# One layer of a hybrid decoder: the outputs of the DeltaNet heads are transposed in 32x32 blocks on VectorE and put in place by transfers through DRAM

## The chip, the cores and the metric

The kernel runs on one core of a Trainium2 chip. The time is that of one execution on the device, in microseconds (us). Before the change three runs gave 1203.46, 1204.15 and 1205.03; the median is 1204.15. The names of the engines are those of the profile: PE is the matrix engine (TensorE) and PEld its loads of weights, DVE is VectorE, ACT is ScalarE, POOL is GpSimd, SP is SyncE, which issues the transfers (SPq is its queue). L139 is line 139 of the kernel. Most instructions are recorded at a helper's line: L139 and L141 are the wrappers of the engines (L141 those with high priority), L191 is a product, L195 a transpose on PE, L200 a transpose of half a block.

## The reference, cut to what matters

The input has 1024 tokens of width 1024, all in float32. The layer is

```
h   = rmsnorm(x);  proj = h @ w_in
o_a = gated_delta_rule(q, k, v, g, beta)          # 4 heads of 128
o_a = rmsnorm(o_a, gdn_norm_w) * silu(z_a)        # per head and token
o_b = dilated_attention(q_b, k_b, v_b)            # 8 heads of 64
x   = x + concat(o_a, o_b) @ w_out
h   = rmsnorm(x);  u = causal_dwconv(h @ w_up)
x   = x + (silu(gate) * up) @ w_down
out = rmsnorm(x)
```

The change touches the second line of o_a: the output of each DeltaNet head is scaled per token by its norm and per feature by gdn_norm_w, multiplied by silu of a projection z, and enters the output projection.

## The kernel before, in words

Activations are held transposed: features on the 128 partitions, the 1024 tokens along the free dimension, in 8 chunks of 128. A product in full precision is made of three fast ones: both operands are split into a high part (a copy rounded to fp32r, on ACT) and a low part (the rest, on DVE: `split`, L209), and `mm3` (L203) multiplies high with high, low with high and high with low. I call these three products of 128x512 a triple. The weights come from DRAM as wst and are split into whi and wlo.

The program is written as generators that a planner (class Weave, L46) interleaves. It keeps a clock of PE and an estimate of when each tile is ready, by fixed and per-element costs for each engine (L148 to L156), and takes the stream with the lowest level that is ready. This gives PE a written order of instructions, which the hardware keeps. The order on DVE, ACT and SP is made afterwards by a scheduler with priorities; each engine then works in its order and waits where an operand is late.

Around the change there are these streams:

- `dense` (L505), level 9: the columns of the input projection, 128 outputs each, 2 halves of 512 tokens, 8 triples per half. It fills what the other streams leave. The last four columns are z, one per DeltaNet head. Each half is evacuated from PSUM by DVE with the token norm rstdB (`scaled`, L444): xr for z, aqkv for the attention.
- `chain` (L789), level 1: the recurrence of one DeltaNet head over 8 chunks of 128 tokens, all four heads interleaved. Each step goes PE, DVE (r, wke, the state ct), ACT (w, vtok) and back. Its output vtok has tokens on the partitions and, per chunk, 128 features along the free dimension. At the end ms holds the mean square per token, POOL raises it to the power -0.5 and multiplies vtok by it (L854, L855).
- `finish` (L858), level 1: for each head 8 transposes of 128x128 on PE, 4 into one PSUM bank, then a copy on ACT that scales each feature by gw2 (half of gdn_norm_w) into ot, and a transfer of each half to the DRAM tile mixer[h].
- In `dense`, when z of head h is reached, og is loaded from mixer[h] with one transfer (L548) and the gate is put off: `gate` (L481) makes zz = tanh(xr/2) on ACT, zz = (zz + 1) * xr on DVE, og = og * zz on DVE. With the halved gw2 this is the product with silu.
- `attention` (L904), level 5: scores on PE, softmax on DVE and ACT (sm), transposes of the probabilities on PE (L200), copies of these on DVE and ACT (pt, pb), products with the values, and oT on DVE.
- `mixer_splits` (L1087), level 0: splits og of each DeltaNet head and ot (the attention's outputs, back from mixer) into ohi and olo. They take the slots of xhi and xlo, so each waits for the last product of `dense` that reads that slot.
- `out_proj` (L1115), level 8: products of ohi and olo with the output weights, heads 0 to 3 first.

All transfers named here stand in one queue, SP's, which issues them in order: one that waits holds those behind it.

Of the kernel before, what the change touches and what calls it, by code (L numbers as in the profile page):

```python
# [7 lines left out]
F32 = mybir.dt.float32  # L8
F32R = mybir.dt.float32r
AF = mybir.ActivationFunctionType  # L10
OP = mybir.AluOpType
# [4 lines left out]
P = 128  # L16
# [3 lines left out]
NCH = 8  # L20
# [124 lines left out]
def hybrid_layer(tc, I, out):  # L145
    nc = tc.nc
    wv = Weave()
    ve = Engine(wv, nc.vector, "vector", 0.07, 0.00105)  # L148
    ac = Engine(wv, nc.scalar, "scalar", 0.12, 0.00085)
# [3 lines left out]
    po_ = Engine(wv, nc.gpsimd, "gpsimd", 0.15, 0.0021)  # L153
    sy = Engine(wv, nc.sync, "sync", 0.05, 0.00142, 2.2)

    sa = Engine(wv, nc.scalar, "sync", 0.05, 0.00142, 2.2)  # L156
    es = ExitStack()
    cp = es.enter_context(tc.tile_pool(name="cp", bufs=1))
# [2 lines left out]
    sp = es.enter_context(tc.tile_pool(name="sp", bufs=1))  # L161
# [3 lines left out]
    def tile_(pool, shape, dt, name, tag, bufs):  # L165
        return wv.slot(pool.tile(list(shape), dt, name=name, tag=tag, bufs=bufs), tag, bufs)
# [3 lines left out]
    def A(name, tag, dt=F32, shape=(P, 1024)):  # L170
        if tag in TURNS:
            i = turns[tag] = turns.get(tag, -1) + 1
            tag = TURNS[tag][i % len(TURNS[tag])]
        return tile_(lp, shape, dt, name, tag, SLOTS[tag])

    def X(name, dt=F32R):
        return A(name, "X", dt)

    def const(name, shape, src=None):
        t = cp.tile(list(shape), F32, name=name)  # L180
        if src is not None:
            sy.dma_start(t, src)
        return t
# [3 lines left out]
    def after(inst, anchor, reason="keeps a slot free until it is needed"):  # L187
        tc.add_manual_dep(inst.ins, anchor.ins.name, order, reason=reason)
# [5 lines left out]
    def tp(dst, src):  # L194
        tc.stamp_issue_order_token(nc.tensor.transpose(dst, src, ident).ins, TOKEN)  # L195
        wv.product(0.11, dst, src)
# [12 lines left out]
    def split(src, hi, lo):  # L209
        ac.activation(hi, src, AF.Copy)  # L210
        return ve.tensor_tensor(lo, src, hi.bitcast(F32), op=OP.subtract)

    def raw_weight(src, n=1024):
        st = tile_(wp, [P, n], F32, "wst", "wst", 2)
        sy.dma_start(st, src)
        return st
# [11 lines left out]
    def wk(src, st=None):  # L228
        return [t.rearrange("p (k m) -> p k m", k=KT) for t in weight(src, st=st)]
# [12 lines left out]
    mixer = dp.tile([8, P, S], F32, name="mixer")  # L242
# [10 lines left out]
    def bank(tag, name="ps"):  # L253
        return tile_(pp_, (P, 512), F32, name, tag, 2)

    def next_bank(tag, *tiles, slack=0.0):

        while max(wv.need(*tiles), wv.slot_free(tag, 2)) + slack > 1e-3:
            yield max(wv.need(*tiles), wv.slot_free(tag, 2)) + slack
        return bank(tag)  # L260

    def half(i):
        return slice(i * 512, i * 512 + 512)
# [80 lines left out]
    gw2 = const("gw2", [P, 1])  # L344
# [23 lines left out]
    rstdB = const("rstdB", [P, S])  # L368
# [75 lines left out]
    def scaled(pair, name, by_class=False, tag="ev", t=None, hs=(0, 1)):  # L444
        if t is None:
            t = A(name, tag)
        for h in hs:
            sl = half(h)
            if by_class:
                ve.tensor_tensor(t[:, sl].rearrange("p (n c u) -> p n u c", n=4, c=4),  # L450
                                        pair[h].rearrange("p (n u c) -> p n u c", n=4, c=4),
                                        rstdB[:, sl].rearrange("p (n u c) -> p n u c", n=4, c=4), op=OP.mult)
            else:
                ve.tensor_tensor(t[:, sl], pair[h], rstdB[:, sl], op=OP.mult)
        return t
# [22 lines left out]

    put_off = []

    def gate(og, xr, anchor=None):  # L481
        y = A("zz", "ev")
        insts = [ac.activation(y, xr, AF.Tanh, scale=0.5),
                 ve.scalar_tensor_tensor(y, y, 1.0, xr, op0=OP.add, op1=OP.mult),
                 ve.tensor_tensor(og, og, y, op=OP.mult)]
        last["og"] = insts[2:]
        if anchor is not None:
            after(insts[0], anchor[0], "the softmax goes first")
            after(insts[1], anchor[1], "the softmax goes first")
# [6 lines left out]
    gated = {}  # L496

    def first_keys():
        xr = [scaled(pst[2 * h:2 * h + 2], "xr", tag=("ev", "ev", "qa")[h]) for h in range(3)]
        for h in range(3):  # L500
            T["k", h] = conv_silu(xr[h], 4 + h, "kT", "kT*")
            wv.add(3, kprep(h))
            yield wv.need(T["k", h])

    def dense():  # L505

        yield from wv.until("first")
        yield from wv.until("norms")
        wv.add(2, first_keys())

        raw = [raw_weight(I["wi"][0])]
        nxt = wk(None, raw.pop())
        raw.append(raw_weight(I["wi"][1]))
        for i, col in enumerate(DENSE):
            kind, h = col[:2]
            if kind == "z":
                yield from wv.until(("o", h))
            w = nxt
            if i + 1 < len(DENSE):
                nxt = wk(None, raw.pop())  # L520
            if i + 2 < len(DENSE):
                raw.append(raw_weight(I["wi"][i + 2]))
            pair = []
            for hh in range(2):
                pt = bank("hf")
                yield wv.need(pt, *w)
                for k in range(KT):
                    mm3(pt, [t[:, k, :] for t in w], [t[:, half(hh)] for t in xs[k]], k == 0, k == KT - 1)
                    yield 0.0

                pair.append(pt)
                if hh == 0:
                    while put_off:
                        gate(*put_off.pop(0))
                    xr = A("aqkv" if kind == "a" else "xr", "go" if kind == "k" else "ev")
                scaled(pair, "xr", kind == "a", t=xr, hs=(hh,))
            if kind == "k":
                T["k", h] = conv_silu(xr, 4 + h, "kT", "kT*")
                wv.add(3, kprep(h))
            elif kind == "q":  # L540
                q = conv_silu(xr, h, "qT", "qa")
                wv.add(4, qprep(h, q))
            elif kind == "v":
                v = conv_silu(xr, 8 + h, "vT", "qa")
                wv.add(4, vprep(h, v))
            elif kind == "z":
                og = gated[h] = A("og", "kT*")
                sy.dma_start(og, mixer[h])  # L548
                if i + 1 < len(DENSE):
                    put_off.append((og, xr))  # L550
                else:
                    gate(og, xr)
            else:
                sy.dma_start(apark[h, col[2]], xr)
                wv.done.add(col)
        wv.done.add("dense")
# [299 lines left out]
        wv.add(1, finish(h, vtok))  # L856

    def finish(h, osb):  # L858
        for hh in range(2):
            pt = yield from next_bank("atr", osb, slack=0.8)  # L860
            for c in range(4):
                i = 4 * hh + c
                tp(pt[:, c * P:(c + 1) * P], osb[:, i * P:(i + 1) * P])
            ot = tile_(sp, [P, 512], F32, "ot", "t2", 2)
            ac.activation(ot, pt, AF.Copy, scale=gw2)
            sy.dma_start(mixer[h][:, half(hh)], ot)
        wv.done.add(("o", h))


# [208 lines left out]
    ots = {}  # L1078
# [4 lines left out]
    def load_residual(m):  # L1083
        x1[m] = A("x1", "kT")
        sy.dma_start(x1[m], I["xT"][m * P:(m + 1) * P, :])

    def mixer_splits():  # L1087
        yield from wv.until("dense")
        load_residual(MORDER[0])
        load_residual(MORDER[1])  # L1090
        wv.done.add("residual")
        for i in range(8):
            yield from wv.until(("o", i))
            ots[i] = (X("ohi"), X("olo"))
            if i < H:
                lo = split(gated[i], *ots[i])
                last.setdefault("olo", []).append(lo)
                if i and "probabilities" in last:
                    after(lo, last["probabilities"], "the probabilities go first")
            else:  # L1100
                src = A("ot", "ev")
                for h in range(2):
                    sl = half(h)
                    if i < 7 or h == 0:
                        sy.dma_start(src[:, sl], mixer[i][:, sl])
                    split(src[:, sl] if i < 7 or h == 0 else last["oT"], *[t[:, sl] for t in ots[i]])
            yield wv.need(*ots[i])
            wv.done.add(("ot", i))
# [656 lines left out]
```

## Time and profile before

| what | value |
|---|---|
| median of three runs | 1204.15 us |
| the profiled execution | 1202.61 us |
| its span | 1200.8 us |
| granted PE clock | 0.998 |
| ACT, share of the span | 48% |
| POOL, share of the span | 5% |
| transfers of mixer<-ot | 8 of 256 KB, 3.1 us to landing |
| transfers of og<-mixer | 4 of 512 KB, 4.2 us to landing |

The span is the time between the first and the last instruction in the trace; the execution is 1.81 us longer. A row of the timeline gives start, duration, engine, line, operation, output and inputs, the number of merged instructions and, in brackets, the idle time of the engine just before and what ended it. A row of a tile gives minimum, median and maximum duration in ns and the first and last start. Matmuls overlap, so their durations add up to more than the time they take.

### The profile page before, as it was taken

The page shows a single profiled execution, that of the slowest core. Times are in us where ns is not written, and L with a number is a line of the kernel's source. Part 1 is how long each engine was busy: PE and PEld are TensorE (multiplying, and loading weights), DVE is VectorE, ACT ScalarE, POOL GpSimd, SP SyncE. Part 2 cuts the span into 40 slices and gives each one's busy share as a digit, 9 for nine tenths or more (in the row PEclk, how much of TensorE's full clock was granted, in tenths as well). Part 3 has the DMA queues.
Part 4 walks back from the last instruction along what each step waited for, and adds up shares of the span by engine and source line. Part 5 has one row for each costly group of instructions (what it writes and reads, how often), then busy time and mean ns, then how long its engine had stood idle before and what let it go on. Part 6 is the DMA issues. An engine that isn't in the chain of part 4 may idle for free.

```text
span 1200.8 us, 18366 instructions
## 1 busy us (share of the span) xinstructions
PE 1190.4 (99%) x7058; PEld 986.1 (82%) x7058; DVE 956.5 (80%) x1532; ACT 575.3 (48%) x1129; POOL 57.1 (5%) x50
## 2 busy tenths in 40 slices
PE   9999999999999999999999999999999999999997
PEld 7888888898777778888888888888888888888887
DVE  7686985483666678767898988989898889898987
ACT  7383344364344445555544544444454454445452
POOL 0212010023000000000000000000000000000001
PEclk9999999999999999999999999999999999999999
DMA  6323234426442313443223222131222395356724
GB/s 237 106 75 102 83 115 129 150 85 238 134 134 84 115 58 124 166 141 122 69 72 106 74 85 102 56 106 53 106 86 72 98 377 217 113 183 218 241 98 157
DMA packets 81704, 152.72 MB, mean 127 GB/s; under 512 B 21552, under 2 KB 32592, under 8 KB 81616
## 3 DMA queue, kind: packets, MB, share of 16 engines
q1 hardware_dynamic: 80896, 151.02, 37.7%
q8 instruction: 55, 0.90, 0.3%
q10 hardware_dynamic: 720, 0.53, 0.1%
q14 instruction: 33, 0.27, 0.1%
HBM read 113.49 MB, written 35.93 MB: 124 GB/s over the span
## 4 chain that ended last, share of the span: by engine, by line
PE 96%; DVE 2%; ACT 1%; DMA 1%; issue 0%; POOL 0%; DVEq 0%; SPq 0%; ACTq 0%; POOLq 0%
PE ps L191 46%; PE pa L191 20%; PE dw L191 17%; PE pc L191 10%; PE ps L195 2%; PE ps L200 1%; DMA wst<-in_wu 0%; ACT sm L141 0%; DVE x1h L139 0%; DMA xt<-in_xT 0%; DVE sm L141 0%; DVE aqkv L139 0%; DVE T L139 0%; DVE wst L139 0%; DVE pair L139 0%
## 5 line engine op out<-in xcount | busy, mean ns | idle before, releaser
L191 PE MATMUL dw<-pr 128*128 128x512 f32 (+1 forms) x984 | 211.4, 376 | 0.0
L191 PEld LDWEIGHTS dw<-pr 128*128 128x128 f32 x984 | 176.7, 188 | 33.6
L191 PE MATMUL ps<-xhi,whi 128*128 128x512 f32 x448 | 184.5, 412 | 0.0
L191 PE MATMUL ps<-xhi,wlo 128*128 128x512 f32 x448 | 175.2, 391 | 0.0
L191 PE MATMUL ps<-xlo,whi 128*128 128x512 f32 x448 | 174.9, 390 | 0.1
L191 PE MATMUL pa<-T,pair 128*128 128x512 f32 x528 | 127.1, 389 | 0.2
L191 PEld LDWEIGHTS pa<-T,pair 128*128 128x128 f32 x528 | 99.0, 188 | 21.2 <-ACT u L139 0.7
L191 PEld LDWEIGHTS ps<-xhi,whi 128*128 128x128 f32 x448 | 84.3, 188 | 19.2 <-issue 3.6
L191 PEld LDWEIGHTS ps<-xhi,wlo 128*128 128x128 f32 x448 | 84.1, 188 | 18.4
L191 PEld LDWEIGHTS ps<-xlo,whi 128*128 128x128 f32 x448 | 84.4, 188 | 14.6 <-DVE xlo L139 0.4
L139 ACT ACTIVATE u<-pa 128x512 f32<-128x512 f32 x44 | 26.3, 598 | 109.7 <-PE pa L191 109.7
L139 DVE SCALAR_TENSOR_TENSOR y<-xu,fcw,y 128x1023 f32<-128x1023 f32 (+1 forms) x44 | 56.3, 1281 | 24.4 <-ACT y L139 24.4
L139 ACT ACTIVATE pr<-wd 128x1024 fp32r<-128x1024 f32 x33 | 35.0, 1061 | 76.1 <-DVE wd L139 39.5
L139 ACT ACTIVATE whi<-wst 128x1024 fp32r<-128x1024 f32 (+2 forms) x38 | 38.5, 1014 | 57.5 <-PE ps L191 48.3
L191 PE MATMUL pa<-B,A 128*128 128x512 f32 x264 | 63.5, 389 | 0.0
L191 PE MATMUL pa<-T,S 128*128 128x512 f32 x264 | 63.4, 389 | 0.0
L191 PE MATMUL pc<-B,pair 128*128 128x512 f32 x264 | 63.4, 389 | 0.0
L191 PE MATMUL pc<-T,S 128*128 128x512 f32 x264 | 63.4, 389 | 0.0
L139 DVE TENSOR_TENSOR wst<-wst 128x512 f32<-128x512 f32 x88 | 60.4, 686 | 0.8
L191 PE MATMUL ps<-B,pair 128*128 128x512 f32 x252 | 60.5, 389 | 0.0
L191 PEld LDWEIGHTS pc<-B,pair 128*128 128x128 f32 x264 | 49.6, 188 | 10.3
L191 PEld LDWEIGHTS pa<-T,S 128*128 128x128 f32 x264 | 49.6, 188 | 10.3
(244 smaller groups left out, 2234.7 us busy)
## 6 DMA issues: line engine op xcount, KB each, us to landing
wst<-in_wu SPq DMA_DIRECT2D x44, 512.0 KB, 3.5
wd<-in_wd SPq DMA_DIRECT2D x44, 512.0 KB, 4.3
wst<-in_wi SPq DMA_DIRECT2D x25, 512.0 KB, 3.6
upark<-y SPq DMA_DIRECT2D x22, 512.0 KB, 3.5
r<-upark SPq DMA_DIRECT2D x22, 512.0 KB, 9.4
apark<-aqkv SPq DMA_DIRECT2D x12, 512.0 KB, 2.8
wa<-in_wd SPq DMA_DIRECT2D x22, 256.0 KB, 2.9
wst<-in_wo SPq DMA_DIRECT2D x8, 512.0 KB, 3.9
```

The lines of the kernel that those rows point to most:

```text
L139: return getattr(eng, op)(*a, **kw)
L191: tc.stamp_issue_order_token(nc.tensor.matmul(dst, lhs, rhs, start=start, stop=stop, **kw).ins, TOKEN)
L195: tc.stamp_issue_order_token(nc.tensor.transpose(dst, src, ident).ins, TOKEN)
L200: tc.stamp_issue_order_token(nc.tensor.transpose(dst, src[rows], ident[rows, rows]).ins, TOKEN)
```

## The change

`finish` no longer uses PE and ACT. DVE transposes all of vtok at once in 32x32 blocks: within each block of 32 partitions and 32 elements, rows and columns are exchanged, and the blocks of one chunk are written so that ft holds, per partition, 4 groups of 256 elements. One transfer stores ft to mixer[h]. The blocks themselves are brought to their partitions by the load: og is now loaded with four transfers of 32 partitions, each from pieces of 256 elements (1 KB).

After this the tokens of og lie in another order along the free dimension: 4 groups of 32 within a chunk come first (`by_row`), where before they followed the token's number (`by_token`). So xr of a z column is written by DVE in that block order, the gate works in it, and the split into ohi and olo reads og by rows and writes the tokens back in their order, with a pattern of 4x8x32. The scaling by gw2 has moved into the last operation of the gate, which is a scalar_tensor_tensor now. The planner counts each of the four loads with 0.05 us + 0.00036 us per element (`sq_`). All else follows from the planner and the scheduler.

```diff
+    sq_ = Engine(wv, nc.sync, "sync", 0.05, 0.00036, 2.2)
...
+    def by_row(t):
+        return t.rearrange("p (a c i) -> p a c i", a=4, c=NCH)
+
+    def by_token(t):
+        return t.rearrange("p (c a i) -> p a c i", a=4, i=32)
+
     def gate(og, xr, anchor=None):
         y = A("zz", "ev")
         insts = [ac.activation(y, xr, AF.Tanh, scale=0.5),
                  ve.scalar_tensor_tensor(y, y, 1.0, xr, op0=OP.add, op1=OP.mult),
-                 ve.tensor_tensor(og, og, y, op=OP.mult)]
+                 ve.scalar_tensor_tensor(og, og, gw2, y, op0=OP.mult, op1=OP.mult)]
...
-                scaled(pair, "xr", kind == "a", t=xr, hs=(hh,))
+                if kind == "z":
+                    ve.tensor_tensor(by_row(xr)[:, :, 4 * hh:4 * hh + 4], by_token(pt), by_token(rstdB[:, half(hh)]), op=OP.mult)
+                else:
+                    scaled(pair, "xr", kind == "a", t=xr, hs=(hh,))
...
                 og = gated[h] = A("og", "kT*")
-                sy.dma_start(og, mixer[h])
+                for b in range(4):
+                    sq_.dma_start(og[32 * b:32 * b + 32].rearrange("j (a y) -> j a y", a=4),
+                                 mixer[h].rearrange("(a j) (b y) -> b j a y", a=4, b=4)[b])
...
     def finish(h, osb):
-        for hh in range(2):
-            pt = yield from next_bank("atr", osb, slack=0.8)
-            for c in range(4):
-                i = 4 * hh + c
-                tp(pt[:, c * P:(c + 1) * P], osb[:, i * P:(i + 1) * P])
-            ot = tile_(sp, [P, 512], F32, "ot", "t2", 2)
-            ac.activation(ot, pt, AF.Copy, scale=gw2)
-            sy.dma_start(mixer[h][:, half(hh)], ot)
+        yield wv.need(osb, slack=0.8)
+        t = A("ft", "kt")
+        ve.transpose(t.rearrange("p (b c i) -> p b c i", b=4, c=NCH), osb.rearrange("p (c b j) -> p b c j", c=NCH, b=4))
+        sy.dma_start(mixer[h], t)
         wv.done.add(("o", h))
...
             if i < H:
-                lo = split(gated[i], *ots[i])
+                g4, hi4, lo4 = by_row(gated[i]), by_token(ots[i][0]), by_token(ots[i][1])
+                ac.activation(hi4, g4, AF.Copy)
+                lo = ve.tensor_tensor(lo4, g4, hi4.bitcast(F32), op=OP.subtract)
```

## The prediction

> **What bounds the kernel now.** I read the page's busy times and its chain first, then the busy time by stretches.
>
> ```profile
> span 1200.8 us, 18366 instructions
> ...
> PE 1190.4 (99%) x7058; PEld 986.1 (82%) x7058; DVE 956.5 (80%) x1532; ACT 575.3 (48%) x1129; POOL 57.1 (5%) x50
> ...
> PE 96%; DVE 2%; ACT 1%; DMA 1%; issue 0%; POOL 0%; DVEq 0%; SPq 0%; ACTq 0%; POOLq 0%
> ```
>
> ```profile
> 225.00:271.00 46.00, 44.94 (x322) 41.33 (x321) 33.89 (x105) 27.33 (x108) 7.53 (x6) 1.00 0.30 101
> 425.00:470.00 45.00, 44.82 (x460) 34.81 (x457) 37.52 (x83) 21.32 (x53) 0.31 (x1) 1.00 0.20 63
> ```
>
> The columns of the second view are stretch, length, then the busy time of PE, PEld, DVE, ACT and POOL, and the granted clock. TensorE is busy 1190.4 of 1200.8 us, and 96% of the chain is its own. In the recurrence it is idle 1.06 us (46.00 less 44.94), in the end of the attention 0.18. So a matmul taken away is time saved, and there is no idle time on PE to hide a new wait in. PE runs in a fixed order: what makes one product late makes all later ones late.
>
> The profiled execution took 1202.61 us, 1.81 more than its span. The median of the three runs is 1204.15, 1.54 above it; I make the sum against the profiled execution and put it onto the median.
>
> **What goes from PE.**
>
> ```profile
> L195 PE MATMUL ps<-ident,vtok x32: 272/273/273, 271.1 to 297.5; 128*128 128x128 f32 x32
> L139 ACT ACTIVATE ot<-ps,gw x8: 667/688/692, 271.7 to 298.0; 128x512 f32<-128x512 f32 x8
> ```
>
> ```profile
> 296.78 1.04 PE L195 MATMUL ps<-ident,vtok 128*128 128x128 f32 x8
> 297.58 0.47 PE L191 MATMUL ps<-xhi,whi 128*128 128x512 f32 x1
> 297.89 0.39 PE L191 MATMUL ps<-xlo,whi 128*128 128x512 f32 x1
> 298.12 0.40 PE L191 MATMUL ps<-xhi,wlo 128*128 128x512 f32 x1
> ```
>
> A transpose shows 0.273 us, but they overlap: eight in a row hold PE from 296.78 to 297.58, and the step after them is 0.31 instead of 0.23. That is 0.80 + 0.08 = 0.88, or 0.11 each, and 32 x 0.11 = **3.5 us**. The eight copies on ACT (8 x 0.688 = 5.5 us) go too, but ACT is busy for only 48% of the span, and no wait of PE above ends with them, so I count nothing for them.
>
> The orders of the two built programs, set against each other, show what fills the holes: between the recurrence's steps stand single dense triples (three products of 0.23, 0.69 us) where the transposes were. That makes three more changes from the recurrence's fp32 products to the dense ones, 0.08 each: **+0.2**. Nine more triples stand ahead of the attention's start and eleven fewer behind its last product (13 before, 2 after).
>
> **What comes onto DVE.** Four block transposes of 128x1024. The trace has none, so I bound one from the nearest rows.
>
> ```profile
> L139 DVE TENSOR_TENSOR og<-og,zz x4: 1211/1214/1225, 429.2 to 472.4; 128x1024 f32<-128x1024 f32 x4
> L139 DVE TENSOR_TENSOR olo<-og,ohi x4: 1218/1222/1226, 465.2 to 474.7; 128x1024 fp32r<-128x1024 f32 x4
> L139 DVE TENSOR_TENSOR xr<-ps,rstdB x32: 677/691/692, 44.4 to 469.1; 128x512 f32<-128x512 f32 x32
> L139 DVE TENSOR_TENSOR aqkv<-ps,rstdB x24: 1036/1106/1146, 67.6 to 395.7; 128x512 f32<-128x512 f32 x24
> L141 DVE COPY pt<-ps x64: 263/415/425, 311.8 to 457.2; 128x256 f32<-128x256 f32 x56, 128x128 f32<-128x128 f32 x8
> ```
>
> ```profile
> 453.57 0.82 DVE L141 TENSOR_SCALAR sm<-sm,mx 128x448 f32<-128x448 f32 x2
> ```
>
> A plain pass over 1024 elements takes 1.22. The costliest pattern, aqkv's scatter of single elements, takes 1.106 for 512 against xr's 0.691, so 2.2 for 1024. The two scalings of sm, one input each, take 0.82 for 2 x 448, or 0.94 for 1024; that is the other end. I take 1.22, and 1.13 from start to start: its runs are 32 elements, and the copies of pt in runs of 64 (256 elements in 0.415) show no such penalty. The same choice stands for xr (0.69), the splits (1.22) and the gate's product (the same length with one more operand) in block order. [...]
>
> Where they stand decides. The first stands in DVE's order behind ms at 266.87 and ahead of vtok, aqkv and wke:
>
> ```profile
> 266.87 0.96 DVE L141 TENSOR_SCALAR ms<-ms 128x8 f32<-128x8 f32 x1 [0.27 <-ACT osq L141]
> 267.50 0.35 DVE L141 SCALAR_TENSOR_TENSOR vtok<-ps,gq,vtok 128x128 f32<-128x128 f32 x1
> 267.80 1.13 DVE L139 TENSOR_TENSOR aqkv<-ps,rstdB 128x512 f32<-128x512 f32 x1
> 268.76 0.33 DVE L141 TENSOR_SCALAR wke<-ps,ke 128x128 f32<-128x128 f32 x1
> 269.25 1.22 DVE L139 TENSOR_TENSOR wlo<-wst,whi 128x1024 fp32r<-128x1024 f32 x1
> 270.38 0.35 DVE L141 SCALAR_TENSOR_TENSOR ct<-ct,ge,ps 128x128 f32<-128x128 f32 x1
> ```
>
> ```profile
> 265.45 1.90 POOL L139 TENSOR_TENSOR vtok<-vtok,ms 128x1024 f32<-128x1024 f32 x1
> ...
> 269.63 2.59 POOL L139 TENSOR_TENSOR vtok<-vtok,ms 128x1024 f32<-128x1024 f32 x1
> ```
>
> ```profile
> 269.45 0.49 PE L191 MATMUL ps<-wke,ktok 128*128 128x128 f32 x2
> 270.79 0.49 PE L191 MATMUL ps<-ct,kT 128*128 128x128 f32 x2 [0.18 <-DVE ct L141]
> ```
>
> DVE has no gap from 267.5 to 270.6, and PE already waits there, for wke and then for ct. The transpose can start at 267.5, when POOL's product of head 0 is through. Everything behind it moves by 1.13, and PE's product on ct with it: **+1.1**.
>
> Then a second effect. POOL's second product took 2.59 instead of 1.90; it starts at 269.63, inside wlo (269.25 to 270.38): 0.69 too long, about what is left of wlo. The 0.96 of ms, an operation on 8 elements, fits the other direction: it waits for POOL's product to end at 267.35. So the two engines exclude each other for some operations. With wlo moved to 270.38, POOL comes first, 269.63 to 271.53, and wlo starts 1.15 later: ct is then at 272.65 and PE's product near 273.0 instead of 270.79: **+1.1** more. [...] If POOL does not hold wlo back, this term is 0; I keep 0 to 1.1.
>
> The second transpose stands ahead of vtok and r, and its input is ready by then; the extra triple in PE's order covers it (r at about 274.9, PE's product on it at 275.3). The third waits for POOL behind ms of head 2, PE reaches the next wke about 0.3 later than it is ready. The fourth follows POOL's last product and falls into the time where DVE idles for 5.26 us between the halves of a column:
>
> ```profile
> 299.94 1.15 DVE L139 TENSOR_TENSOR aqkv<-ps,rstdB 128x512 f32<-128x512 f32 x1 [5.26 <-PE ps L191]
> ```
>
> Together **+0.1**, at most 1.2 if one is not covered.
>
> **SP's queue.** Per head, one store instead of two and four loads of og instead of one; the first load waits for its store, and behind it stand weight loads.
>
> ```profile
> 290.20 0.38 SPq L139 DMA_DIRECT2D wst<-in_wi  x1
> ```
>
> ```profile
> wst<-in_wi SPq DMA_DIRECT2D x25, 512.0 KB, 3.6
> ```
>
> ```profile
> 299.70 1.06 ACT L139 ACTIVATE whi<-wst 128x1024 fp32r<-128x1024 f32 x1 [1.02 <-PE ps L191]
> ```
>
> The weight load at 290.20 lands 3.6 later, 5.9 us before its split. The issue at 290.20 takes 0.38, so three more are 1.1 us; og itself is first used at 429.2, by its row above. So 0; a load later than that would cost what exceeds the 5.9.
>
> **The end of the attention.** Thirteen dense triples (8.9 us) stand there now behind the last product of the attention; two (1.4 us) will.
>
> ```profile
> 456.24 1.41 DVE L141 COPY pt<-ps 128x256 f32<-128x256 f32 x4
> ...
> 469.07 0.69 DVE L139 TENSOR_TENSOR xr<-ps,rstdB 128x512 f32<-128x512 f32 x1 [0.40 <-PE ps L191]
> ```
>
> ```profile
> 468.87 0.39 PE L191 MATMUL ps<-ohi,whi 128*128 128x512 f32 x1
> 469.81 0.50 PE L191 MATMUL ps<-ohi,whi 128*128 128x512 f32 x1
> 471.26 0.50 PE L191 MATMUL ps<-ohi,wlo 128*128 128x512 f32 x1
> ```
>
> PE now loses 0.26 at 469.81, for the last xr to free its bank, and 0.2 at 471.26 for a weight split: 0.45. In the new order DVE does zz, olo and xr between the last sm (454.4) and the copies of pt, which then end at 458.8 (454.4 + 1.15 + 1.15 + 0.65 + 1.4); og, two olo and oT follow (458.8 + 1.15 + 2.3 + 1.0), so the last xr runs from 463.2 to 463.9. PE reaches the dense end near 462.2, its next bank at 462.9, and waits to 463.9: 1.0, and 0.2 for the copies of pt. Against the 0.45 of now: **+0.7**, between 0 and 1.5.
>
> **Sum:** -3.5 + 0.2 + 1.1 + 1.1 + 0.1 + 0.7 = -0.3 us: 1202.3 for the profiled execution, and on the median 1204.15 - 0.3 = **1203.9**. A measurement of this kernel can tell about 0.2% (2.4 us) from no change, so this is the same.
>
> **Rivals.** (1) *The saving arrives.* The waits in the recurrence and at the end are absorbed: -3.5 + 0.2 = -3.3, 1200.9. For it: the planner set those triples where DVE is loaded. Against it: PE already waits for wke and ct there, and one exposed transpose takes a third of it. With the transpose exposed and nothing else, it is -2.2, 1202.0, still the same. (2) *Block order is dear on DVE.* If runs of 32 cost as aqkv's single elements do (1.6 times), the first transpose adds 1.0, olo and xr ahead of pt's copies 1.1, two olo and xr behind them 1.9: 4.0 more, 1207.9, slower. For it: aqkv. Against it: pt. From about 1.4 times it decides the sign. (3) *A load is late*: a column's weights behind the waiting og loads, beyond their 5.9 us. For it: the first of the four waits for a store, on a queue in order. Against it: the stores now go out in one piece. A load 9 us later than now would stop PE for 3.1: 1207.0, slower. That the change does not do what it says is no rival: the built order holds no transpose of vtok on PE.
>
> **Chances.** Forecast 0.55, rival 1 0.20, rival 2 0.17, rival 3 0.08. So faster by over 0.2% 0.20, within 0.2% 0.55, slower by over 0.2% 0.25. The range, 1201.0 to 1207.2, takes in most of rival 1, a transpose of 2.2 us and part of rival 2.
>
> **What would show it.** In the new profile: PE without the 32 transposes and 3.5 us less busy; the block transpose at 1.2 us (0.94 or 2.2 if I chose the wrong row); PE's wait on ct near 273 and wlo beginning only when POOL is done; POOL's second product at 1.90 instead of 2.59; a wait of about 1 us behind the last xr. I am wrong if PE idles elsewhere in the attention, or if olo and xr in block order are not 1.22 and 0.69.

## The result and the profile after

The changed kernel takes 1206.59 us (median of 11 runs, 1205.65 to 1208.73), the kernel before 1203.11 in runs beside it (11 runs). The ratio is 1.003, with a 95% interval of 1.0022 to 1.0037: 3.5 us slower. I had forecast 0.3 us less, which is no change. The profiled execution took 1206.25 us, 3.64 more than that of before. Of most kernels here some executions take about 2 us longer than the rest at a lower mean granted clock (of 21 of the kernel before, run beside e10, four took 1205.1 to 1205.3 us at 0.995 to 0.997 and the others 1202.3 to 1203.9 at 0.997 or 0.998), so that a median of few can fall on either side.

The page of the changed kernel, the same rows as before:

```profile
span 1204.5 us, 18283 instructions
...
PE 1189.4 (99%) x7026; PEld 983.8 (82%) x7026; DVE 962.1 (80%) x1536; ACT 571.0 (47%) x1121; POOL 54.5 (5%) x50
...
PE 93%; DVE 4%; ACT 1%; DMA 1%; issue 1%; POOL 0%; DVEq 0%; SPq 0%; ACTq 0%; POOLq 0%
```

The 32 transposes are gone from PE (7026 matmuls instead of 7058), but PE is busy for only 1.0 us less, and the chain now goes through DVE for 4% instead of 2%. The waits of PE name the places (engine, line, what ended the wait: sum, times, longest):

```profile
PE ps L201 <- DVE sm L141: 2.0, 3, 0.9
PE ps L192 <- DVE ct L141: 1.8, 2, 1.4
PE ps L192 <- ACT w L141: 1.3, 2, 0.8
...
PE ps L196 <- ACT pb L141: 0.5, 1, 0.5
```

Of these, before the change only ct and w were waited for:

```profile
PE ps L191 <- DVE ct L141: 0.6, 2, 0.4
PE ps L191 <- ACT w L141: 0.5, 1, 0.5
```

PE's order is fixed, so I can set the two traces against each other and take out the triples that stand earlier or later (0.68 us each: in the rows of before, eight steps of dense products from 466.83 to 468.64 take 1.81, 0.226 each). What is then left is the time lost or won up to that point. The first row rests on these two (before, then changed), with 311 triples ahead of the one and 320 ahead of the other:

```profile
304.51 1.03 PE L195 MATMUL ps<-ident,vT 128*128 128x128 f32 x8
...
309.42 1.03 PE L196 MATMUL ps<-ident,vT 128*128 128x128 f32 x8
```

| up to | triples earlier | shift | net |
|---|---|---|---|
| first transposes of vT in the attention (304.51, now 309.42) | +9 | +4.91 | -1.21 |
| next transposes of vT (332.92, now 338.74) | +9 | +5.82 | -0.30 |
| scores of the last softmax (448.31, now 455.35) | +10 | +7.04 | +0.24 |
| first product of the output projection (468.87, now 472.44) | 0 | +3.57 | +3.57 |

So the recurrence ended as forecast (-1.0 by my sum, -1.2 measured), and then three places in the attention took 0.9, 0.5 and 3.3 us.

**The recurrence.** DVE and POOL of the changed kernel:

```profile
267.46 1.25 DVE L139 STREAM_TRANSPOSE ft<-vtok 128x1024 f32<-128x1024 f32 x1
...
270.27 2.41 DVE L139 TENSOR_TENSOR wlo<-wst,whi 128x1024 fp32r<-128x1024 f32 x1
272.61 0.34 DVE L141 SCALAR_TENSOR_TENSOR ct<-ct,ge,ps 128x128 f32<-128x128 f32 x1
...
269.71 1.90 POOL L139 TENSOR_TENSOR vtok<-vtok,ms 128x1024 f32<-128x1024 f32 x1
```

This is the forecast row for row: the transpose at 267.5, POOL's product at 1.90 again, wlo held from 270.3, ct at 272.6, PE's product on it at 273.00. The block transpose and the pass in block order have the prices I took:

```profile
L139 DVE STREAM_TRANSPOSE ft<-vtok x4: 1229/1245/1245, 267.5 to 296.3; 128x1024 f32<-128x1024 f32 x4
```

```profile
L139 DVE TENSOR_TENSOR olo<-og,ohi x4: 1217/1221/1227, 465.4 to 478.4; 128x1024 fp32r<-128x1024 f32 x4
```

**The start of the attention.** A table load of 1.28 us stands on ACT ahead of the first exp of the softmax. Before the change that load had no wait and ran as soon as vn was copied (first fence); in the changed kernel it stands behind the wait for the softmax on DVE (second fence), and exp comes 1.30 later (314.64 instead of 313.34). PE waits 0.56 for sm at 317.15.

```profile
306.25 1.28 ACT L141 ACT_TABLE_LOAD   x1
308.49 0.40 ACT L141 ACTIVATE sm<-sm,mx 128x128 f32<-128x128 f32 x1 [0.96 <-DVE mx L141]
```

```profile
313.34 1.28 ACT L141 ACT_TABLE_LOAD   x1 [1.92 <-DVE mx L141]
314.64 0.41 ACT L141 ACTIVATE sm<-sm,mx 128x128 f32<-128x128 f32 x1
```

The list of waits in the built program says why. ACT used to copy the transposes of vtok, so it had waited for PE, which had waited for POOL. Now ACT has never waited for POOL when it first writes sm, into space that POOL had written. That exp needs two waits, on DVE and on POOL, and the build puts the one on DVE ahead of the table load, which stands directly ahead of that exp.

**The end of the attention.** DVE, ACT and PE of the changed kernel, in the order of time on each:

```profile
453.76 1.40 DVE L141 COPY pt<-ps 128x256 f32<-128x256 f32 x4
458.74 1.23 DVE L139 TENSOR_TENSOR wlo<-wst,whi 128x1024 fp32r<-128x1024 f32 x1 [3.58 <-ACT whi L139]
459.88 0.58 DVE L141 CUSTOM_DVE_ANT_0 sm<-ps,mk 128x416 f32<-128x416 f32 x1
```

```profile
457.59 1.06 ACT L139 ACTIVATE whi<-wst 128x1024 fp32r<-128x1024 f32 x1 [2.12 <-DMA wst<-in_wo]
```

```profile
462.77 0.71 PE L201 MATMUL ps<-ident,sm 64*128 64x64 f32 x16 [0.86 <-DVE sm L141]
464.07 0.73 PE L201 MATMUL ps<-ident,sm 64*128 64x64 f32 x16 [0.59 <-DVE sm L141]
464.73 0.77 PE L192 MATMUL ps<-xhi,whi 128*128 128x512 f32 x1
465.30 0.63 PE L192 MATMUL ps<-xlo,whi 128*128 128x512 f32 x1
465.72 0.63 PE L192 MATMUL ps<-xhi,wlo 128*128 128x512 f32 x1
```

Read from the DMA to PE: the weights of the third output column land at 457.5. Their low part stands in DVE's order ahead of the last softmax, so DVE idles 3.58 us for it although the scores are there at about 457.0, and the softmax begins at 459.88. PE stands 0.86 and 0.59 us for sm. And then its products come every 0.43 us instead of every 0.23. The view by stretches shows the granted clock (the column behind POOL's):

```profile
461.00:464.70 3.70, 2.25 (x37) 1.63 (x35) 3.33 (x11) 3.70 (x10) 0.00 (x0) 1.00 0.47 136
464.70:468.20 3.50, 3.50 (x12) 2.78 (x9) 3.50 (x7) 2.04 (x6) 0.00 (x0) 0.51 0.17 40
468.20:471.70 3.50, 3.50 (x53) 2.96 (x52) 3.50 (x4) 1.82 (x6) 0.00 (x0) 1.00 0.33 115
```

For 3.41 us the clock is at half (0.51 in the view), so the products in it take 1.7 us longer by estimate (half of 3.41), and the view counts PE as busy all that time (3.50 of 3.50). This is one reason why PE's busy time fell so little: in e6 and e8 below, whose profiles have no such stretch, it is 1188.5 and 1188.3. Whether the stretch costs time at the end is asked under p1.

In the kernel before, that low part stood behind the last softmax (the first row is the start of that softmax):

```profile
449.97 0.59 DVE L141 CUSTOM_DVE_ANT_0 sm<-ps,mk 128x416 f32<-128x416 f32 x1 [2.10 <-PE ps L191]
...
461.94 1.21 DVE L139 TENSOR_TENSOR wlo<-wst,whi 128x1024 fp32r<-128x1024 f32 x1
```

The chain for its space (whi of an earlier column, its wlo, the load) starts when a dense column ends, and that whi is at 454.00 there and at 450.64 here. That this is why the scheduler turned the two around is my reading; no run shows it.

### The profile page after: what moved, and what is told of

Its sections match the earlier page's. It is cut to its first block, busy times and chain, and to the rows that moved or that the text cites. A ratio compares the mean times of both kernels' runs of the same rounds, so it can differ in the third digit from the quotient of the medians.

```text
span 1204.5 us, 18283 instructions
## 1 busy us (share of the span) xinstructions
PE 1189.4 (99%) x7026; PEld 983.8 (82%) x7026; DVE 962.1 (80%) x1536; ACT 571.0 (47%) x1121; POOL 54.5 (5%) x50
## 4 chain that ended last, share of the span: by engine, by line
PE 93%; DVE 4%; ACT 1%; DMA 1%; issue 1%; POOL 0%; DVEq 0%; SPq 0%; ACTq 0%; POOLq 0%
PE ps L192 44%; PE pa L192 19%; PE dw L192 17%; PE pc L192 10%; PE ps L196 1%; PE ps L201 1%; DVE sm L141 1%; DMA wst<-in_wu 0%; ACT sm L141 0%; DVE wlo L139 0%; DVE x1h L139 0%; DMA wst<-in_wo 0%; DVE oT L139 0%; DMA xt<-in_xT 0%; DVE pt L141 0%
## 5 line engine op out<-in xcount | busy, mean ns | idle before, releaser
L192 PEld LDWEIGHTS pc<-T,S 128*128 128x128 f32 x264 | 49.5, 188 | 10.3
```

The lines of the kernel that those rows point to most:

```text
L192: tc.stamp_issue_order_token(nc.tensor.matmul(dst, lhs, rhs, start=start, stop=stop, **kw).ins, TOKEN)
```

## The experiments

My theory after the two traces: the saving on PE is real; the loss is made of waits, each from the order of instructions on DVE or ACT, in the recurrence by the block transposes, in the attention by the triples that moved and by the lost wait for POOL. The rivals: the saving was never there; or DVE simply has too much work (80% busy), so that no order helps. Except for b1 and p1, all kernels are the changed kernel with another order on DVE, a wait of POOL (e6) or one small copy on ACT (e2, e9, e10); PE's order is the same in all of these, instruction for instruction, and in b1 too. Ratios are to the kernel before, run beside each (medians 1203.1 to 1203.4).

| kernel | median us | ratio, 95% interval |
|---|---|---|
| the change | 1206.59 | 1.0030, 1.0022 to 1.0037 |
| e1, softmax first | 1205.41 | 1.0016, 1.0007 to 1.0025 |
| e2, POOL seen | 1207.13 | 1.0027, 1.0017 to 1.0037 |
| e3, two transposes later | 1208.30 | 1.0039, 1.0027 to 1.0051 |
| e6, POOL after wlo | 1208.01 | 1.0030, 1.0018 to 1.0042 |
| e7, all transposes later | 1204.57 | 1.0013, 1.0004 to 1.0022 |
| e8, end in order | 1204.25 | 1.0012, 1.0003 to 1.0021 |
| e9, all of these | 1200.58 | 0.9976, 0.9966 to 0.9986 |
| b1, before without transposes | 1203.57 | 1.0004, 0.9995 to 1.0013 |
| e10, e9 and og later | 1201.52 | 0.9983, 0.9975 to 0.9992 |
| e11, e10 without the look at POOL | 1202.08 | 0.9990, 0.9981 to 0.9999 |

**e1: the last softmax ahead of the late weights.**

```diff
-                ends = softmax(it)
+                ends = last["ends"] = softmax(it)
...
-                split(raw_weight(I["wo"][MORDER[2]]), *third)
+                after(split(raw_weight(I["wo"][MORDER[2]]), *third), last["ends"][1], "the last softmax goes first")
```

> The changed kernel, with one edit: on DVE the low part of the third output column's weights (it was late because its load landed at 457.5) stands behind the last softmax instead of ahead of it. My theory: this low part held the last softmax back by 2.9 us (it began at 459.88, its scores were there at about 457.0); PE waited 0.86 + 0.59 for sm, and after these waits its granted clock was 0.51 for 3.5 us, in which nine products took 0.43 instead of 0.23. So the two waits and the slow stretch go: 1.45 + about 1.7 = 3.1 us, 1206.6 becomes about 1203.5, no faster than 1203.1 of before. Rival A: the wait only moves, to the copies of pt or to the last xr behind it: the gain is under 1 us, 1205.6 or more. Rival B: the slow clock is not a consequence of the waits: the gain is the 1.45 alone, about 1205.1, and the granted clock near 465 stays 0.5.

Measured: 1205.41, 1.2 less: rival A, mostly. The two waits for sm and the slow stretch at the end are gone, and the ninth dense product behind them starts 3.3 us earlier, counted from the scores. (The profiled execution has another slow stretch, from 572.86 to 576.27; see p1.) But DVE now does wlo, zz and olo between the softmax and the copies of pt, and PE waits there and for the last xr:

```profile
466.54 0.66 PE L192 MATMUL ps<-pt,vn 128*64 128x128 f32 x8 [0.70 <-DVE pt L141]
467.80 0.66 PE L192 MATMUL ps<-pt,vn 128*64 128x128 f32 x8 [0.60 <-DVE pt L141]
...
472.86 0.50 PE L192 MATMUL ps<-ohi,whi 128*128 128x512 f32 x1 [0.82 <-DVE xr L139]
```

**e8: the whole end in order.**

```diff
+                after(last["zz"], inst, "the probabilities go first")
...
-                if i and "probabilities" in last:
+                if "probabilities" in last:
...
+                    after(last["og"][0], last["xr"], "the last z goes first")
...
-                split(raw_weight(I["wo"][MORDER[2]]), *third)
+                after(split(raw_weight(I["wo"][MORDER[2]]), *third), last["olo"][-1], "the heads go first")
```

> The changed kernel, with DVE's order at the end of the attention written down: the last softmax, then the copies of pt, then zz, olo, the xr's, og, and the third column's low part last. Theory: nothing but this order makes PE wait there. The waits for sm (0.86 + 0.59), for pt (0.70 + 0.60 when only the softmax came first) and most of that for the last xr (0.32 to 0.82) go, and with them the stretch at half clock: 1206.6 becomes 1203.0 to 1203.6. Rival: DVE simply has too much work there (zz, og and the two first olo, 4.6 us); PE waits for olo or xr instead and the time is 1205 or more.

Measured: 1204.25, 2.3 less, between the two expectations. No wait for sm, pt or xr is left at the end; one of 0.88 for wlo of the second output column stands there instead. So most of the end's loss was order, not the amount of work: 2.3 of 3.3.

**e2: ACT looks at POOL's output early.**

```diff
+        if h == H - 1:
+            seen = tile_(sp, [P, 8], F32, "seen", "r1", 1)
+            ac.activation(seen, osb[:, :8], AF.Copy)
```

> The changed kernel, with one more operation: behind the last block transpose ACT copies 8 elements of vtok into a spare tile, so that ACT has waited for POOL once by then. Theory: in the kernel before, ACT waited for the transposes of vtok on PE, which waited for POOL; so the first exp of the attention had one wait, on DVE, and the table load ahead of it (1.28 us) ran early. In the changed kernel ACT has not waited for POOL, the exp needs two waits, one of them stands at the table load, and the load runs only at 313.34, when the softmax is ready. The copy removes that: the load runs right behind vn, PE no longer waits 0.56 and 0.4 for sm near 316 to 317, and 1206.6 becomes about 1205.5 (-1.0). Rival: the load stays where it is or another wait ends as late, no change, 1206.6.

Measured: 1207.13. The mechanism is shown: with one copy of 8 elements the table load runs right behind vn again, without a wait, and PE no longer waits for sm at 316.

```profile
313.50 1.28 ACT L141 ACT_TABLE_LOAD   x1
315.36 0.40 ACT L141 ACTIVATE sm<-sm,mx 128x128 f32<-128x128 f32 x1 [0.58 <-DVE mx L141]
```

The gain is not to be seen in the median: in the profiled execution the clock fell to half from 273.25 to 276.67, behind the waits for w and ct (1.4 us lost by the attention's start against the changed kernel), and at the end PE waited 0.81 for pt and 0.81 for xr. Three of the eight executions, at a mean clock of 0.997 or 0.998, took 1205.37 to 1205.45; the three of the changed kernel at 0.998 took 1205.65 to 1206.35. e11 below asks again where the waits at the end are gone.

**e3 and e7: the block transposes out of the recurrence.** e3 put the transposes of heads 0, 1 and 2 behind ms of the next head; e7 all three behind ms of the last:

```diff
-        uv.tensor_scalar(ms, ms, 1.0 / 128, EPS, op0=OP.mult, op1=OP.add)
+        chain_end[h] = uv.tensor_scalar(ms, ms, 1.0 / 128, EPS, op0=OP.mult, op1=OP.add)
...
+        if h == H - 1:
+            for i in range(H - 1):
+                after(turns_[i], chain_end[H - 1], "the recurrence goes first")
```

> The changed kernel, with the block transposes of heads 0, 1 and 2 placed on DVE behind the end of the recurrence (ms) of the head after them. Theory: the first transpose, 1.13 us in DVE's order ahead of aqkv, wke and ct, and POOL's product that then came ahead of wlo and held it for 1.2, cost PE 2.2 us near 270 to 273; with the transpose later DVE's order there is that of before, so these waits go, 1206.6 becomes about 1204.4 (-2.2). Rival: the transposes cost the same at their new places because DVE has no free time in the recurrence: 1206 to 1207. A smaller second effect that could come with either: the transfers of mixer start later, which has room of tens of us.

Measured: 1208.30, with the waits of 0.79 and 1.37 unchanged. This run tells little: ms of head 1 already stood ahead of the first transpose, so only the second and third moved, and these are not the ones that cost.

> The changed kernel, with the block transposes of heads 0, 1 and 2 on DVE behind the last operation of the whole recurrence (ms of head 3); in the run before this only the second and third had moved, since ms of head 1 already stood ahead of the first. Theory: the first transpose in its place of 267.5 causes both waits of PE, 0.79 for w and 1.38 for ct (the second with the lock on wlo). With DVE's order there as before the change, they fall to the 0.18 of before: 2.0 us less, 1206.6 becomes about 1204.6. Rival: later waits (for sm, pt, xr near 463 to 474) take the 2 us back: 1206 or more, while the waits near 270 to 273 are gone all the same.

Measured: 1204.57, 2.0 less, as the theory said. The wait for ct near 271 is 0.18 as before the change, that for w is gone. The three transposes run back to back behind the recurrence, where DVE has nothing else to do. The waits at 463 to 474 stayed (sm, pt, xr: 0.70, 0.58, 0.85, 0.81).

**e6: POOL's product behind wlo.**

```diff
-        po_.tensor_tensor(v8(vtok), v8(vtok), ms[:, :, None].to_broadcast([P, NCH, P]), op=OP.mult)
+        normed[h] = po_.tensor_tensor(v8(vtok), v8(vtok), ms[:, :, None].to_broadcast([P, NCH, P]), op=OP.mult)
...
+        tc.add_manual_dep(normed[1].ins, lows_made[15].ins.name,
+                          mybir.DependencyInfo(mybir.DependencyClass.Sync, mybir.DependencyReason.DATA),
+                          reason="the weights go first")
```

> The changed kernel, with POOL's product of head 1 made to wait for the wlo that it held back near 270; the block transpose of head 0 stays where it is, that of head 1 moves behind one r. Theory of the lock (the two engines exclude each other while both work on SBUF): wlo takes 1.22 instead of 2.41, ct and PE's product on it come about 1.1 earlier, 1206.6 becomes about 1205.5 to 1205.8. Rival: the 2.41 has another cause, for instance the weights' split not being ready: wlo stays at 2.4 and the time at 1206.6.

Measured: 1208.01, no gain in the median of five; but that POOL's product held wlo is shown. With that product behind it wlo takes 1.22 instead of 2.41, and the wait for ct falls from 1.38 to 0.18.

```profile
270.36 1.22 DVE L139 TENSOR_TENSOR wlo<-wst,whi 128x1024 fp32r<-128x1024 f32 x1
...
271.72 1.90 POOL L139 TENSOR_TENSOR vtok<-vtok,ms 128x1024 f32<-128x1024 f32 x1 [2.00 <-DVE wlo L139]
```

In the changed kernel POOL's product ran from 269.71 to 271.61, and wlo, begun at 270.27, ended at 272.68. That is shown for this pair of operations; which others hold each other, and why, no run shows. Part of the wait came back, because the second transpose now waits for the later product and holds the next ct:

```profile
271.89 0.49 PE L192 MATMUL ps<-ct,kT 128*128 128x128 f32 x2 [0.18 <-DVE ct L141]
...
275.18 0.49 PE L192 MATMUL ps<-ct,kT 128*128 128x128 f32 x2 [0.53 <-DVE ct L141]
```

The five times of e6 fall into two groups, 1205.5 twice and 1208.0 to 1208.3 three times; the profiled one (1205.48) has no stretch of low clock. The two show a mean clock of 0.998, the three 0.997. One stretch at half clock (1.7 us of 1205, or 0.0014, by the estimate above) would fit both differences, but the traces of the three are not at hand.

**b1: the kernel before, without the transposes.** It leaves out the transposes of vtok, their copies and the scaling by gw2.

```diff
-        for hh in range(2):
-            pt = yield from next_bank("atr", osb, slack=0.8)
...
-            ac.activation(ot, pt, AF.Copy, scale=gw2)
-            sy.dma_start(mixer[h][:, half(hh)], ot)
+        yield wv.need(osb, slack=0.8)
+        for hh in range(2):
+            sy.dma_start(mixer[h][:, half(hh)], osb[:, half(hh)])
```

> The kernel before, with the work left out: the 32 transposes of vtok on PE, their 8 copies on ACT and the scaling by gw2; vtok is stored as it is, in the same 8 transfers. Nothing is added on DVE. The planner then sets the dense triples as in the changed kernel, and DVE's order at the end of the attention has the late low part of the weights ahead of the last softmax, as there. If the saving of PE is all that counts: 1203.2 - 3.5 = 1199.7. If the moved triples alone already bring the waits at the end of the attention (about 3 us, with the half clock): 1202 to 1203, with waits for sm near 460 and none near 270. If the saving is not there at all: 1203.2 with no new waits.

Measured: 1203.57, no different from before (0.9995 to 1.0013), though 3.5 us of work on PE are left out and nothing is added. At the attention's start PE is 3.43 us ahead (net of nine triples); at the output projection it is 0.35 behind. Its waits are those of the changed kernel, without the recurrence's and the table load's:

```profile
PE ps L200 <- DVE sm L141: 1.4, 2, 0.8
...
PE ps L195 <- ACT pb L141: 0.5, 1, 0.5
...
PE ps L191 <- DVE xr L139: 0.3, 1, 0.3
```

So the moved triples, with the order that the scheduler then gives the other engines and without any block transpose, lose 3.8 us: the whole saving.

**e9: all orders together.** e7, e2 and e8, and zz behind the copies of pt in the middle of the attention:

```diff
+        if anchor is None and "copy" in last:
+            after(insts[1], last["copy"], "the probabilities go first")
```

> The changed kernel with all of these: block transposes behind the recurrence, ACT's early look at POOL's output, zz behind the copies of pt in the middle of the attention and the written order at its end. PE's order is that of the changed kernel, instruction for instruction. Theory: the saving of 3.5 us on PE is there all along, and the changed kernel lost it to the waits of DVE's and ACT's order: about 2.0 + 1.0 + 0.5 + 3.1 us go, 1206.6 becomes 1199.8 to 1200.5, about 3 us under before. Rival: the saving was never there (the triples that took the holes cost as much): 1203 with hardly a wait of PE left.

Measured: 1200.58, 0.24% under before (0.14 to 0.34%), 6.0 us under the change. The page and the waits of e9:

```profile
PE 1187.3 (99%) x7026; PEld 982.7 (82%) x7026; DVE 960.8 (80%) x1536; ACT 570.7 (48%) x1122; POOL 55.2 (5%) x50
```

```profile
PE ps L192 <- DVE wlo L139: 0.9, 1, 0.9
PE ps L192 <- DVE ct L141: 0.6, 2, 0.4
PE ps L192 <- ACT w L141: 0.5, 1, 0.5
```

PE is busy for 3.1 us less than before, and only one wait is new, the 0.88 for wlo. Net of triples PE is 3.48 ahead at the attention's start and 3.61 at the output projection. The rival that the saving was never there falls.

**e10 and e11: the last wait, and the table load by itself.** e10 is e9 with og of the third head behind that wlo instead of behind the last xr; e11 is e10 without ACT's copy of 8 elements.

```diff
+        after(gate_og[0], lows_made[-1], "the first weights go first")
```

> The kernel with all orders, and og of the third head behind the low part of the second output column's weights on DVE. Theory: the one wait that was left, 0.88 us for that low part, falls to the 0.2 of the kernel before, and 1200.6 becomes 1199.7 to 1199.9: the full 3.5 us under before. Rival: an olo or the last xr is late instead, 1200.6.

> The same kernel without ACT's early look at POOL's output; everything else is the same instruction for instruction. Theory: the table load of 1.28 us stands behind the softmax of the attention's first pair again, PE waits about 1.0 for sm near 313 and the time is 1.0 over the run beside it, about 1200.8. Rival: later waits, or the slack of PE, swallow it: the same time as the run beside it, within 0.3.

Measured: e10 1201.52. This is the rival's mechanism, and 0.9 over its time: the wait for wlo is gone, but og is later and PE waits for two olo, 0.55 and 0.49. That DVE has no room left there is not shown, since it idles ahead of the first of these olo, for a tanh (zz) that ACT does ahead of the ohi which that olo needs:

```profile
470.17 1.23 DVE L139 SCALAR_TENSOR_TENSOR zz<-zz,xr 128x1024 f32<-128x1024 f32 x1 [1.13 <-ACT zz L139]
```

```profile
469.07 1.06 ACT L139 ACTIVATE zz<-xr 128x1024 f32<-128x1024 f32 x1 [2.49 <-DVE og L139]
470.04 1.05 ACT L139 ACTIVATE ohi<-og 128x1024 fp32r<-128x1024 f32 x1
```

No run tried the other order on ACT. e11 1202.08, 0.56 more than e10: its table load stands at 311.30 behind 1.92 of waiting, PE waits 0.56 for sm at 315.10, and at 422 it is 0.84 behind e10's. The time moves in the direction of the theory by about half of the 1.0; the two intervals overlap, so the trace, more than the time, carries this term.

**p1: forced waits.** The kernel before with 46 forced pauses of PE, each one to three tiny products that ACT must read:

```diff
+                for _ in range((1, 2, 3)[(2 * i + hh) % 3] if i > 1 else 0):
+                    tc.stamp_issue_order_token(nc.tensor.matmul(pt[:, :8], xs[0][0][:, :P], xs[0][0][:, :8],
+                                                                start=True, stop=True).ins, TOKEN)
+                    ua.activation(warm2, pt[:, :8], AF.Copy)
```

> The kernel before with waits forced on PE: ahead of each half of a dense column (from the third column on) one, two or three tiny products, each of which the ACT engine reads before the next may start, so that PE stands nearly idle for some 0.7, 1.4 or 2.1 us at 46 places. It is not timed for itself; it asks how often a wait is followed by products of 0.43 instead of 0.23. If a wait's length alone decides, all of the long ones are followed by a slow stretch and none of the short ones. If it depends on where the wait falls in a period that runs by itself (the clock that was low after waits of 1.3 to 1.45 us in three profiles and not in three others), a part of the long ones is, and of the same length some are and some aren't.

Measured, from the end of the product or transpose ahead of the tiny ones to the start of the next: of 30 pauses under 1.7 us none was followed by a slow stretch; of 16 of 1.78 and more, 11 were. Two pauses of nearly one length, 3.17 and 3.15 us, with what follows:

```profile
545.40:548.90 3.50, 1.09 (x8) 0.83 (x5) 2.34 (x6) 1.40 (x7) 0.00 (x0) 1.00 0.02 7
548.90:552.00 3.10, 3.10 (x10) 2.40 (x10) 0.00 (x0) 0.00 (x0) 0.00 (x0) 0.59 0.00 0
...
438.30:441.80 3.50, 0.90 (x5) 0.51 (x5) 3.39 (x10) 2.60 (x10) 0.00 (x0) 1.00 0.19 76
441.80:445.00 3.20, 3.20 (x24) 2.42 (x25) 0.38 (x1) 0.00 (x0) 0.00 (x0) 1.00 0.71 232
```

The clock falls behind the one and not behind the other. The changes of the clock are recorded in the traces. Between two of them the clock was full for a whole multiple of 3.413 us (460.80, or 135 of them, in the changed kernel; 1191.25, or 349, in the one before; 566.61, or 166, in e1) and at half for 3.41 us (464.79 to 468.20 in the changed kernel, 572.86 to 576.27 in e1), or for two of these behind the pause of 6.69 in p1. I call 3.413 us a step and count from the changes. The first pause then has 2.57 us inside one step, and the clock falls where that step ends (549.47); the second is split into 1.73 and 1.43. All 11 pauses with a fall have 1.78 us or more in one step; of the other 35 only one has (1.93). Where the steps lie differs from one profiled execution to the next: the first recorded change is at 3.99 us in the changed kernel, at 4.51 in the one before.

In the changed kernel PE has 2.8 us without a 128x512 product (461.91 to 464.73), about half of it the last transposes of sm. In the profiles of the change, e3 and b1 the whole of this stretch lies in one step, and the clock fell; in those of e2, e6 and e7 the steps cut it, with at most 2.4 in one, and it did not. But here the fall costs nothing that shows, because without it PE waits 0.8 for pt and 0.8 for xr instead: from the scores of the last softmax to the 100th instruction of PE behind the first product of the output projection it is 40.43, 40.27 and 40.28 us in the three with the fall and 40.36, 40.31 and 40.26 in the three without. What the end loses there is the late softmax.

Elsewhere a fall does cost. Near 565 to 573 every kernel here, the one before too, has 1.5 to 2.3 us without a 128x512 product, with sixteen of 128x1 in it. In the profiles of e1, e10 and e11 all of it, 1.9 to 2.1 us, lay in one step and the clock fell behind it; in the others at most 1.8 us did, and it did not fall. In those three, 300 instructions of PE around it took 67.6 us, against 65.7 to 66.4 in the other profiles of this order of PE.

## Why the prediction was wrong

The time lies in the range, near its upper end, but on the other side of no change than the forecast. Even that is luck: the range was put on a median of 1204.15, and on the 1203.11 of the runs beside it would have ended at 1206.2. By the terms of its sum:

| term | forecast | measured |
|---|---|---|
| transposes gone, switches added | -3.3 | -3.43 (b1; -3.48 in e9) |
| first transpose exposed, and wlo held | +2.2 | +2.22 (the change against b1 at the attention's start) |
| other three transposes | +0.1 | none seen |
| ACT's copies gone | 0 | +0.91 (table load) |
| triples moved, middle of the attention | 0 | +0.54 (pb) |
| end of the attention | +0.7 | +3.33 |
| sum | -0.3 | +3.57 (+3.64 at the end of the executions) |

**Right:** the 0.11 of a transpose, the 1.22 of a block transpose and of the passes in block order (rival 2 is out: nothing cost 1.6 times), the place of the first transpose, that POOL's product holds wlo (2.41, against 1.22 in e6), and that SP's four loads per head do no harm (og is there 100 us before its use). One reading was wrong without changing the sum: before the change PE did not wait for wke (its row at 269.45 has no wait), only for ct (0.18); in the changed kernel it waits 0.79 there (put down to w).

**Wrong first: the end of the attention.** The step failed where it says that "DVE does zz, olo and xr between the last sm (454.4) and the copies of pt". I left the last softmax at its old time and worked only behind it. But DVE's new order, which I had, has a wlo ahead of that softmax, and this wlo waits for a load. The load is issued when the wlo before it frees its space (453.84 in the new trace). Rows of before have the rest: 3.6 for the load, 1.06 for whi and 1.14 for wlo are 5.8 us from the end of that wlo to the end of this one, and the softmax stands behind it, at 459.6 or later (459.88 measured), with its scores there since about 457.0. So the softmax began 2.9 us late, and with the end's order written down (e8) 2.3 of the 3.3 us came back. It resembles rival 3, a late load; but the load was not late behind og on SP's queue. It could start no sooner, and an instruction that needed it stood ahead of one that did not.

**Wrong second:** "The eight copies on ACT go too ... so I count nothing for them." They carried a wait. With them went ACT's knowledge that POOL was done, and the table load lost its head start: 0.91 us.

**Not counted, but not the cause:** the half clock behind a pause was in none of my terms, since the trace of before has no such stretch (full clock for 1191.25 us, from 4.51 to 1195.76). In the changed kernel the clock fell to half for 3.41 us, and PE was busy for 2.25 of the 3.70 us ahead of that. In e2, e6 and e7 the steps lay otherwise and it did not fall there, and at this place the fall cost nothing that shows (see p1). At the first product of the output projection, where the last row of the table ends, the profiles with the fall are some 0.5 us later than those without, but they wait 0.3 to 0.4 for the xr behind it instead of 0.8.

**What stays open:** whether the half clock is what puts the median of e6 2.5 above its profiled execution (the mean clocks fit, the traces are missing), whether the last waits for olo in e10 are order too, and how much of the 0.9 of the table load reaches the end when nothing behind it waits (0.56 by e11 against e10). That the middle's 0.5 comes from zz and wlo ahead of the copies of pt was tried only together with the rest, in e9, where it is gone.

## What to carry to other kernels

When work leaves the bound engine, the planner's other work moves into its place, and every other engine's order moves with it: go through that order for each instruction that waits for a load and ask what stands behind it, above all where it is ahead of the critical chain. An instruction that is taken away can have carried a wait for others; look at what the next ones wait for now. Here the change pays only with DVE's order written down (and one small copy on ACT): e9 is 2.6 us faster than before, the plain change 3.5 us slower.

## What the runs showed of the hardware

Some pauses of PE cost more than themselves. Between two changes the clock was full for 135 times 3.413 us in the changed kernel, 349 times in the one before and 166 times in e1. Of the 46 pauses of p1 it fell behind 11, each with 1.78 us or more inside one such step (a twelfth had 1.93 there and no fall). The products then came every 0.43 us instead of every 0.23, for one step of 3.41 us, or for two behind the pause of 6.69: up to 1.7 us more per step, an estimate (half of 3.41). Near 570 that cost is seen in full (67.6 us in e1, e10 and e11 against 65.7 to 66.4), at the end of the attention, where PE would have waited anyway, not at all (40.27 to 40.43 against 40.26 to 40.36). A wlo of 128x1024 that began inside POOL's product took 2.41 us in the changed kernel, and 1.22 ahead of that product in e6. Behind a table load (1.28 us) the next exp began 0.02 us later in the changed kernel (313.34 to 314.64), with no further pause.
